# Output-weight remainders on VectorE: one operation of 512 columns or two of 256

## The chip, the cores and the metric

The kernel runs on one core of a Trainium2 chip. The metric is the device time of one execution in microseconds, and the number that counts is the median of the runs. TensorE (PE in the profile) multiplies matrices, VectorE (DVE), ScalarE (ACT) and GpSimd (POOL) do the elementwise work, and SyncE (SP) issues most of the transfers. Every engine works through its own list of instructions in the order in which the program was built, and waits on semaphores for the others.

## The reference

One layer of a model with three parallel mixers. An input of 512 tokens by 1024 channels is normed and projected; the projection feeds a gated linear attention (256 channels), a diagonal state-space mixer (256 channels) and a sparse attention with three branches (512 channels). Their outputs are concatenated and projected back:

```python
h = rmsnorm(x, norm_g[l])
proj = jnp.matmul(h, w_in[l])
...
y_gla = gla_mixer(...)
y_s5 = s5_mixer(...)
y_nsa = nsa_mixer(...)
mix = jnp.concatenate([y_gla, y_s5, y_nsa], axis=-1).astype(x.dtype)
x = x + jnp.matmul(mix, w_out[l])
```

The change lies in the preparation of `w_out`, a 1024 x 1024 float32 matrix, for the last product.

## The kernel before

**Products in three parts.** TensorE takes its operands in a rounded float32 format. To keep accuracy, the kernel splits an operand into a high part (the rounded value) and a low part (the remainder), and sums three products: high times high, high times low, low times high. For the output weights `out_weights` makes the two parts. The matrix lies in eight row blocks k of 128 rows, and each block is handled in two halves of 512 columns (`hf`): SP loads a half into a buffer `wor` (line 1085), ScalarE rounds it into `woh[k]` (line 1086), and the remainder `wor - woh` goes into `wol[k]` (line 1087). The remainder of the first half (`hf` 0) is computed by GpSimd, that of the second half by VectorE; both inputs of the subtraction lie in SBUF. `out_weights(0)` does blocks 0 to 3, `out_weights(1)` blocks 4 to 7, so the line issues eight operations on VectorE and eight on GpSimd. A buffer `wor` comes from a small set of slots that other work uses too; a later load into the slot has to wait until the subtraction has read it.

**Who uses the parts.** `out_first(i)` multiplies the first four row blocks with the mixers' first 512 channels for the 128 tokens of tile i; `out_second(i)` does the last four with the sparse attention's channels and writes the result. Their matmuls stand at line 165, with tiles `pp<-woh,mh`, `pp<-wol,mh`, `pp<-woh,ml` in the first and `moh` in the place of `mh` in the second.

**What runs beside it.** Between 240 and 305 us the kernel works on the attention of the second group of heads. For each unit of it (a tile of 128 queries, a pair of heads, one or two branches): TensorE makes scores `ps`; VectorE takes their maximum `nm` (line 1158); ScalarE takes the exponential into `p` (line 1161); VectorE makes a weighting `dn` from its sum and the branch's gate (lines 1162 and 1163); GpSimd multiplies `p` by `dn` (line 1164; both inputs in SBUF); TensorE transposes `p` into a bank `pt` (line 1182); VectorE or ScalarE, in turn, copies it to `pT` (lines 1186 and 1188); TensorE multiplies `pT` by the values `kvr`. At the end of a pair of tiles VectorE gates the sum into `sng` (line 1213), which frees its bank. In the same stretch a small attention over compressed keys runs, with GpSimd's product at line 1062.

**What sets the order.** Five streams (projection, linear attention, state space, sparse attention, output) are generators, and a string `ORDER` says whose next step is written. The instructions are then placed on the engines' lists by a scheduler that estimates when each would run, so a change of one operation's shape can move others past each other.

Of the kernel before, what the change touches and what calls it, by code (L numbers as in the profile page):

```python
# [8 lines left out]
F32 = mybir.dt.float32  # L9
# [4 lines left out]
OP = mybir.AluOpType  # L14
# [47 lines left out]
def kernel(ctx: ExitStack, tc: tile.TileContext, a: dict, out: bass.AP):  # L62
    nc = tc.nc
    V, S, G, PE = nc.vector, nc.scalar, nc.gpsimd, nc.tensor
# [16 lines left out]
    def al(name, shape, dt=F32, keep=False):  # L81
        size = int(math.prod(shape[1:])) * mybir.dt.size(dt)
        for cls, top, _ in (JOB + CLASSES if any(stack[0] is j for j in job) and not keep and size > 1024 else CLASSES):
            if size <= top and free[cls]:
                slot = free[cls].pop(0)
                t = slots.tile(list(shape), dt, name=name, tag=slot, bufs=1)
                owned[id(t)] = cls, slot, name, t
                if not keep:
                    stack[0][-1].append(t)
                return t  # L90
        raise RuntimeError(f"no slot for {name}: {[(o[0], o[2]) for o in owned.values()]}")
# [23 lines left out]
    @contextmanager  # L115
    def scope():
        st = stack[0]
        st.append([])
        yield
        fr(*[t for t in st.pop() if id(t) in owned])  # L120
# [952 lines left out]
    def out_weights(part):  # L1073
        if part == 0:
            px.close()
            wo = ctx.enter_context(tc.tile_pool(name="wo", bufs=1))
            N["wo"] = [[wo.tile([128, D], F32R, name=f"wo{c}{k}") for k in range(NK)] for c in "hl"]
            N["opart"] = {}
        woh, wol = N["wo"]
        for k in range(4 * part, 4 * part + 4):  # L1080
            for hf in range(2):
                with scope():
                    r = al("wor", (128, 512))
                    c = slice(hf * 512, hf * 512 + 512)
                    nc.sync.dma_start(out=r, in_=a["w_out"][:, k, c])
                    S.activation(woh[k][:, c], r, AF.Copy)
                    (V if hf else G).tensor_tensor(wol[k][:, c], r, woh[k][:, c].bitcast(F32), op=OP.subtract)  # L1087
            yield

    def out_mm(ps, lh, ll, ks, n):  # L1090
# [126 lines left out]
    with scope():  # L1217
# [5 lines left out]
    s5 = Stream(s5_params, s5_in, s5_scan, s5_out_weights, s5_y, s5_glu)  # L1223
    nsa = Stream("cmp_blocks", cmp_mlp, "nsa_q0", "nsa_kv0", (cmp_attn, 0), "nsa_kv1", (attn, 0), "nsa_q1", (cmp_attn, 1), (attn, 1))
    outs = Stream("nsa_gate1", (out_weights, 0), (out_first, 3), (out_first, 2), (out_weights, 1), (out_first, 1), (out_first, 0),
                  "mix11", (out_second, 3), (out_second, 2), "mix10", (out_second, 1), (out_second, 0))
    job.append(outs.stack)
# [108 lines left out]
```

## Time and profile before

| | |
|---|---|
| runs shown | 350.76, 351.85 and 632.46 us, median 351.85 |
| the profiled execution | 348.96 us, of which its span 347.0 us |
| granted TensorE clock | 1.00 over the span |
| busy: PE, VectorE, ScalarE, GpSimd | 333.3, 241.3, 161.9 and 74.7 us |

The profile is one execution, seen by the hardware profiler. Its page names each group of instructions by line, engine, operation, output and inputs. In a timeline a row gives the start, the length, the instruction and, in brackets, how long the engine had been idle before it and whose work ended that. Lengths of one behind another on the same engine overlap a little: the next instruction may start before the record of the one before ends, so what one costs its engine is read from start to start. PE is busy in nearly every slice, but this is a modelled busy time of pipelined matmuls.

### The profile page before, as it was taken

The numbers are of one execution on the slowest core, as the hardware profiler recorded it, in microseconds if no ns is written. First come the engines' busy times: TensorE is split into PE (matmuls) and PEld (weight loads), VectorE is DVE, ScalarE is ACT, GpSimd is POOL, SyncE is SP. The second block draws the span as 40 slices with busy tenths as digits, with TensorE's granted clock in tenths as the row PEclk, the third lists the DMA queues.
The fourth block names the chain that finished last, engine by engine and source line by source line (L and its number), as shares of the span: only waits on it lengthen the run. The fifth ranks groups of instructions, "written<-read, shape, count | busy, mean of one in ns | idle before, by whom it ended". The sixth has DMA issues, their size and how long they took to land.

```text
span 347.0 us, 6782 instructions
## 1 busy us (share of the span) xinstructions
PE 333.3 (96%) x2620; PEld 271.1 (78%) x2620; DVE 241.3 (70%) x502; ACT 161.9 (47%) x355; POOL 74.7 (22%) x74
## 2 busy tenths in 40 slices
PE   8999998999999999999999999999889899899996
PEld 3889987989997767878778877788766687678785
DVE  2839989999995325844759577978998865843422
ACT  3875542358561125622607249634975355732200
POOL 0000232200000000002301041644584335811000
PEclk9999999999999999999999999999999999999999
DMA  6997577133384557621423200121341123500122
GB/s 181 353 358 240 140 233 238 34 117 86 106 258 129 135 161 228 173 56 35 118 72 82 73 0 2 32 53 39 93 124 30 60 63 120 178 7 2 61 91 91
DMA packets 27538, 40.35 MB, mean 116 GB/s; under 512 B 3033, under 2 KB 16738, under 8 KB 27506
## 3 DMA queue, kind: packets, MB, share of 16 engines
q1 hardware_dynamic: 26370, 37.23, 35.7%
q0 software_dynamic: 1136, 2.69, 2.7%
q8 instruction: 20, 0.33, 0.4%
q14 instruction: 12, 0.10, 0.1%
HBM read 33.42 MB, written 3.92 MB: 108 GB/s over the span
## 4 chain that ended last, share of the span: by engine, by line
PE 63%; DVE 18%; DMA 9%; ACT 6%; issue 3%; POOL 1%; SPq 0%; ACTq 0%; DVEq 0%; POOLq 0%
PE pp L165 33%; PE pt L165 14%; PE ps L165 11%; DMA wor<-in_w_out_dram 4%; DVE nm L1158 3%; DVE wol L1087 2%; ACT p L1161 2%; DMA wr<-in_w_kv_dram 2%; PE pt L1182 2%; DMA wr<-in_w_ng_dram 1%; DVE wl L230 1%; DMA xr<-in_xT_dram 1%; DVE pT L1186 1%; DMA wr<-in_w_nq_dram 1%; DVE dn L1163 1%
## 5 line engine op out<-in xcount | busy, mean ns | idle before, releaser
L1164 POOL TENSOR_TENSOR p<-p,dn 128x1024 f32<-128x1024 f32 (+2 forms) x24 | 39.7, 1653 | 48.2 <-DVE dn L1163 42.8
L229 ACT ACTIVATE wh<-wr 128x512 fp32r<-128x512 f32 (+2 forms) x48 | 30.2, 635 | 38.0 <-PE pp L165 13.7
L230 DVE TENSOR_TENSOR wl<-wr,wh 128x512 fp32r<-128x512 f32 (+2 forms) x48 | 34.8, 730 | 18.0 <-ACT wh L229 17.9
L165 PE MATMUL pp<-wh,xh 128*128 128x256 f32 (+2 forms) x160 | 45.6, 288 | 1.5 <-ACT qr L280 1.4
L165 PE MATMUL pp<-wh,xl 128*128 128x256 f32 (+2 forms) x160 | 45.8, 287 | 0.0
L165 PE MATMUL pp<-wl,xh 128*128 128x256 f32 (+2 forms) x160 | 45.7, 286 | 0.0
L1161 ACT ACTIVATE p<-ps,nm 128x512 f32<-128x512 f32 (+3 forms) x64 | 33.2, 532 | 20.1 <-DVE nm L1158 19.1
L165 PE MATMUL pp<-xh,wh 128*128 128x512 f32 x80 | 32.0, 401 | 0.3 <-DVE sgt L285 0.3
L165 PEld LDWEIGHTS pp<-wh,xh 128*128 128x128 f32 x160 | 30.0, 189 | 2.7 <-ACT qr L280 1.6
L165 PE MATMUL pp<-xh,wl 128*128 128x512 f32 x80 | 32.0, 400 | 0.0
L165 PE MATMUL pp<-xl,wh 128*128 128x512 f32 x80 | 32.0, 400 | 0.0
L165 PE MATMUL ps<-kA,qA 128*128 128x512 f32 (+2 forms) x96 | 28.5, 388 | 2.5 <-ACT p L1161 2.5
L165 PEld LDWEIGHTS pp<-wh,xl 128*128 128x128 f32 x160 | 30.1, 188 | 0.7 <-issue 0.6
L165 PEld LDWEIGHTS pp<-wl,xh 128*128 128x128 f32 x160 | 30.2, 189 | 0.4 <-issue 0.2
L1158 DVE TENSOR_REDUCE nm<-ps 128x1 f32<-128x512 f32 (+3 forms) x48 | 27.5, 590 | 3.6 <-PE ps L165 3.5
L165 PE MATMUL pt<-pT,kvr 128*64 128x128 f32 x320 | 22.6, 280 | 2.2 <-DVE pT L1186 2.1
L1182 PE MATMUL pt<-ident,p 128*128 128x128 f32 x160 | 23.4, 278 | 0.5 <-POOL p L1164 0.4
L165 PEld LDWEIGHTS pt<-pT,kvr 128*64 128x64 f32 x320 | 17.0, 136 | 7.4 <-DVE pT L1186 3.4
L1182 PEld LDWEIGHTS pt<-ident,p 128*128 128x128 f32 x160 | 17.5, 141 | 4.5 <-issue 2.4
L165 PEld LDWEIGHTS ps<-kA,qA 128*128 128x128 f32 x96 | 14.8, 190 | 5.6 <-ACT p L1161 4.5
L1020 POOL MEMSET vblk<- 128x512 f32 x1 | 0.5, 524 | 86.0 <-PE pt L165 86.0
L165 PEld LDWEIGHTS pp<-xh,wl 128*128 128x128 f32 x80 | 15.1, 188 | 3.9 <-issue 0.8
(384 smaller groups left out, 758.0 us busy)
## 6 DMA issues: line engine op xcount, KB each, us to landing
w<-in_w_dram SPq DMA_DIRECT2D x16, 256.0 KB, 3.8
wor<-in_w_out_dram SPq DMA_DIRECT2D x16, 256.0 KB, 2.8
xr<-in_xT_dram SPq DMA_DIRECT2D x8, 256.0 KB, 5.9
xn<-in_xn_dram SPq DMA_DIRECT2D x4, 512.0 KB, 7.0
wr<-in_w_kv_dram SPq DMA_DIRECT2D x8, 256.0 KB, 3.8
wr<-in_w_nq_dram SPq DMA_DIRECT2D x8, 256.0 KB, 5.9
wr<-in_w_ng_dram SPq DMA_DIRECT2D x8, 256.0 KB, 3.7
opart<-in_xn_dram SPq DMA_DIRECT2D x4, 512.0 KB, 3.9
```

Source lines behind the costliest of these rows:

```text
L165: PE.matmul(o, lhsT=l, rhs=r, start=start, stop=stop, **kw)
L229: S.activation(hs[qt][:, :, :w], r[:, :, :w], AF.Copy)
L230: V.tensor_tensor(ls[qt][:, :, :w], r[:, :, :w], hs[qt][:, :, :w].bitcast(F32), op=OP.subtract)
L1020: G.memset(vblk, 0.0)
L1087: (V if hf else G).tensor_tensor(wol[k][:, c], r, woh[k][:, c].bitcast(F32), op=OP.subtract)
L1158: V.tensor_reduce(nm[:, e], sv[e], axis=AX.X, op=OP.max, negate=True)
L1161: S.activation(pv[:, e, b], sv[e][:, b], AF.Exp, bias=nm[:, e, b:b + 1], accum_out=dn[:, e, b:b + 1])
L1163: V.tensor_tensor(dn, dn, gates[:, i].rearrange("p (h b) -> p h b", b=3)[:, h:h + 2, 1 + b0:1 + b0 + nb], op=OP.mult)
L1164: G.tensor_tensor(pv, pv, dn[:, :, :, None].to_broadcast([128, 2, nb, n]), op=OP.mult)
L1182: PE.transpose(pb[:, tok(x_)], p[:, e, c:c + 128], ident)
L1186: V.tensor_copy(pt[:, :w], pb[:, :w])
```

## The change

On VectorE the subtraction of a half of 512 columns is written as two operations of 256 columns, the second right behind the first; the values that are computed are the same. GpSimd's eight subtractions stay as they are.

```diff
                     nc.sync.dma_start(out=r, in_=a["w_out"][:, k, c])
                     S.activation(woh[k][:, c], r, AF.Copy)
-                    (V if hf else G).tensor_tensor(wol[k][:, c], r, woh[k][:, c].bitcast(F32), op=OP.subtract)
+                    if hf:
+                        for q in range(2):
+                            c = slice(hf * 512 + q * 256, hf * 512 + q * 256 + 256)
+                            V.tensor_tensor(wol[k][:, c], r[:, q * 256:q * 256 + 256], woh[k][:, c].bitcast(F32),
+                                            op=OP.subtract)
+                    else:
+                        G.tensor_tensor(wol[k][:, c], r, woh[k][:, c].bitcast(F32), op=OP.subtract)
             yield
```

The scheduler places the new operations, and a few others change places. Line numbers from 1087 on rise by six in the changed kernel (1158 becomes 1164), the tile numbers of one and the same step by a few. Three places matter here.

VectorE's list around the third subtraction (row block 2), where `dn` is a weighting and `nm` a maximum; before:

```order
L1163 TENSOR_TENSOR dn_3069<-dn_3069,gates 128x2
L1087 TENSOR_TENSOR wol_3156<-wor,woh_3148 128x512
L1186 COPY pT<-pt_3016 128x512
L1158 TENSOR_REDUCE nm<-ps_3189 128x1
L1162 RECIPROCAL dn_3087<-dn_3087 128x2
L1163 TENSOR_TENSOR dn_3087<-dn_3087,gates 128x2
L1158 TENSOR_REDUCE nm<-ps_3190 128x1
```

and with the change:

```order
L1169 TENSOR_TENSOR dn_3069<-dn_3069,gates 128x2
L1090 TENSOR_TENSOR wol_3156<-wor,woh_3148 128x256 x2
L1192 COPY pT<-pt_3016 128x512
L1164 TENSOR_REDUCE nm<-ps_3192 128x1
L1168 RECIPROCAL dn_3087<-dn_3087 128x2
L1164 TENSOR_REDUCE nm<-ps_3193 128x1
L1169 TENSOR_TENSOR dn_3087<-dn_3087,gates 128x2
```

The two halves stand side by side, and behind them the second maximum has moved ahead of the weighting that GpSimd's product needs.

GpSimd's list around its last subtraction (row block 7), where `p` is the product with the weighting; before:

```order
L1087 TENSOR_TENSOR wol_3160<-wor,woh_3152 128x512
L1164 TENSOR_TENSOR p<-p,dn_3456 128x2x384
L1164 TENSOR_TENSOR p<-p,dn_3493 128x1024
L1087 TENSOR_TENSOR wol_3161<-wor,woh_3153 128x512
L1164 TENSOR_TENSOR p<-p,dn_3631 128x1024
```

and with the change:

```order
L1093 TENSOR_TENSOR wol_3160<-wor,woh_3152 128x512
L1170 TENSOR_TENSOR p<-p,dn_3460 128x2x384
L1093 TENSOR_TENSOR wol_3161<-wor,woh_3153 128x512
L1170 TENSOR_TENSOR p<-p,dn_3497 128x1024
L1170 TENSOR_TENSOR p<-p,dn_3639 128x1024
```

The last subtraction has moved ahead of the first of the two 1024-column products.

TensorE's list at the same time, where `pt<-ident,p` are the transposes of `p`, `pt<-pcT,vb` the first products into a new bank, and `pp` the output products of a tile; before:

```order
L165 MATMUL pt_3129<-pT,kvr_1146 64x128 x6
L1182 MATMUL pt_3652<-ident,p 128x128 x4
L1182 MATMUL pt_3659<-ident,p 128x128 x4
L165 MATMUL pt_3665<-pcT_1894,vb_1811 128x256
L165 MATMUL pt_3665<-pcT_1895,vb_1811 128x256
L165 MATMUL pt_3665<-pcT_1894,vb_1812 128x256
L165 MATMUL pp_3563<-woh_3146,mh 128x512
L165 MATMUL pp_3563<-wol_3154,mh 128x512
```

and with the change:

```order
L165 MATMUL pt_3129<-pT,kvr_1146 64x128 x6
L165 MATMUL pp_3571<-woh_3146,mh 128x512
L165 MATMUL pp_3571<-wol_3154,mh 128x512
L165 MATMUL pp_3585<-woh_3146,mh 128x512
L165 MATMUL pp_3585<-wol_3154,mh 128x512
L1188 MATMUL pt_3660<-ident,p 128x128 x4
L1188 MATMUL pt_3667<-ident,p 128x128 x4
L165 MATMUL pt_3673<-pcT_1894,vb_1811 128x256
```

Four output products have moved ahead of the transposes and of the products into the new bank.

## Rows read from the trace of the kernel before

**Rows 1.** The head of the profile's page: the span, then the busy time of each engine as a share of the span with its number of instructions.

```profile
span 347.0 us, 6782 instructions
...
PE 333.3 (96%) x2620; PEld 271.1 (78%) x2620; DVE 241.3 (70%) x502; ACT 161.9 (47%) x355; POOL 74.7 (22%) x74
```

**Rows 2.** The table by stretches: start and end of the stretch and its length in us, then the busy time (and number of instructions) of PE, the weight loads, DVE, ACT and POOL, the granted TensorE clock as a fraction of full speed, the DMA share and GB/s.

```profile
240.00:305.00 65.00, 59.15 (x473) 47.20 (x473) 53.29 (x102) 39.43 (x122) 36.24 (x24) 1.00 0.31 94
305.00:344.00 39.00, 38.93 (x222) 31.60 (x222) 14.15 (x26) 6.02 (x17) 2.08 (x2) 1.00 0.13 49
```

**Rows 3.** The timeline of PE: start us, length us, engine, line, operation, out<-in, and in brackets the idle time just before with what ended it. The first six rows are waits of PE for VectorE, ScalarE and GpSimd; the last two are the first and the last of four products in a row.

```profile
255.25 0.66 PE L165 MATMUL pt<-pT,kvr 128*64 128x128 f32 x8 [0.49 <-DVE pT L1186]
...
259.79 0.66 PE L165 MATMUL pt<-pT,kvr 128*64 128x128 f32 x8 [1.07 <-DVE pT L1186]
...
266.76 0.63 PE L165 MATMUL ps<-kA,qA 128*128 128x384 f32 x2 [0.54 <-ACT p L1161]
...
291.44 0.88 PE L165 MATMUL pt<-pT,kvr 128*64 128x128 f32 x12 [0.56 <-DVE pT L1186]
...
297.92 0.44 PE L1182 MATMUL pt<-ident,p 128*128 128x128 f32 x2 [0.43 <-POOL p L1164]
...
303.38 0.62 PE L165 MATMUL pt<-pcT,vb 128*128 128x256 f32 x3 [0.37 <-DVE sng L1213]
303.83 0.45 PE L165 MATMUL pp<-woh,mh 128*128 128x512 f32 x1
...
304.58 0.40 PE L165 MATMUL pp<-wol,mh 128*128 128x512 f32 x1
```

**Rows 4.** A piece of the chain of work that ended last: start us, length us, engine, tile, line.

```profile
252.50 1.18 DVE wol L1087
...
253.71 2.81 DMA wor<-in_w_out_dram
...
256.54 0.64 ACT woh L1086
...
257.20 1.93 DVE wol L1087
```

**Rows 5.** The timeline of DVE (columns as in rows 3) at a place where POOL stands still: operations with both inputs in SBUF, one behind the other.

```profile
189.68 0.41 DVE L509 TENSOR_TENSOR ex<-ex,kT 128x256 f32<-128x256 f32 x1
190.02 0.68 DVE L288 SCALAR_TENSOR_TENSOR sgt<-sl_t,sgt 128x512 f32<-128x512 f32 x1
190.62 0.68 DVE L230 TENSOR_TENSOR wl<-wr,wh 128x512 fp32r<-128x512 f32 x1
```

**Rows 6.** The timeline of POOL (columns as in rows 3) where the output weights are split.

```profile
251.84 1.29 POOL L1087 TENSOR_TENSOR wol<-wor,woh 128x512 fp32r<-128x512 f32 x1
253.08 1.49 POOL L1164 TENSOR_TENSOR p<-p,dn 128x512 f32<-128x512 f32 x1
254.77 1.04 POOL L1164 TENSOR_TENSOR p<-p,dn 128x512 f32<-128x512 f32 x1 [0.19 <-DVE dn L1163]
256.69 1.89 POOL L1164 TENSOR_TENSOR p<-p,dn 128x1024 f32<-128x1024 f32 x1 [0.89 <-DVE dn L1163]
258.54 1.72 POOL L1087 TENSOR_TENSOR wol<-wor,woh 128x512 fp32r<-128x512 f32 x1
...
262.85 1.90 POOL L1164 TENSOR_TENSOR p<-p,dn 128x1024 f32<-128x1024 f32 x1 [0.19 <-DVE dn L1163]
...
286.28 1.47 POOL L1164 TENSOR_TENSOR p<-p,dn 128x768 f32<-128x768 f32 x1 [0.99 <-ACT p L1161]
...
296.11 1.76 POOL L1164 TENSOR_TENSOR p<-p,dn 128x768 f32<-128x768 f32 x1 [0.18 <-DVE dn L1163]
298.64 1.89 POOL L1164 TENSOR_TENSOR p<-p,dn 128x1024 f32<-128x1024 f32 x1 [0.78 <-DVE dn L1163]
300.49 1.28 POOL L1087 TENSOR_TENSOR wol<-wor,woh 128x512 fp32r<-128x512 f32 x1
301.93 2.21 POOL L1164 TENSOR_TENSOR p<-p,dn 128x1024 f32<-128x1024 f32 x1 [0.17 <-DVE dn L1163]
```

**Rows 7.** The timeline of DVE (columns as in rows 3) in the same stretch.

```profile
252.42 1.25 DVE L1087 TENSOR_TENSOR wol<-wor,woh 128x512 fp32r<-128x512 f32 x1
...
259.06 0.68 DVE L1186 COPY pT<-pt 128x512 f32<-128x512 f32 x1
...
260.44 0.16 DVE L1163 TENSOR_TENSOR dn<-dn,gates 128x2 f32<-128x2 f32 x1
...
262.25 0.43 DVE L1163 TENSOR_TENSOR dn<-dn,gates 128x2 f32<-128x2 f32 x1
...
263.80 1.49 DVE L1087 TENSOR_TENSOR wol<-wor,woh 128x512 fp32r<-128x512 f32 x1
...
284.66 1.19 DVE L1087 TENSOR_TENSOR wol<-wor,woh 128x512 fp32r<-128x512 f32 x1
...
295.86 0.68 DVE L1087 TENSOR_TENSOR wol<-wor,woh 128x512 fp32r<-128x512 f32 x1
...
300.93 0.85 DVE L1163 TENSOR_TENSOR dn<-dn,gates 128x4 f32<-128x4 f32 x1
301.71 0.68 DVE L1087 TENSOR_TENSOR wol<-wor,woh 128x512 fp32r<-128x512 f32 x1
```

**Rows 8.** The timeline of ScalarE (columns as in rows 3): the last load of output weights for POOL as it is rounded.

```profile
298.69 0.63 ACT L1086 ACTIVATE woh<-wor 128x512 fp32r<-128x512 f32 x1 [0.50 <-DMA wor<-in_w_out_dram]
```

## The prediction, made before the changed kernel was run

> **What bounds the kernel.** The page's head comes first: PE is busy for 333.3 of 347.0 us, VectorE for 241.3, POOL for 74.7 [rows 1]. That says TensorE, but the matter is decided by stretches, so the second view is the table by stretches, cut where the edit lies. From 240 to 305 us, where the output weights are split, PE is busy for 59.15 of 65 us and VectorE for 53.29; from 305 to 344 PE is idle for 0.07 of 39 us, at a granted clock of 1.00 in both [rows 2], the upper of its two levels. So the end is PE work alone, and an edit of VectorE can shift the end only through the 5.85 us of PE idle before 305. The third view, PE's timeline, names who ends that idle time: pT copies of VectorE, exponentials that wait for VectorE's maxima, a product of POOL, a gating of VectorE [rows 3]. What stands on VectorE ahead of those is what counts, and the edited line is among it: the chain of waits runs through it twice within 5 us, by way of the load that its end sets free [rows 4].
>
> The fourth view lays VectorE and POOL side by side. An operation of 512 columns with both inputs in SBUF is 0.68 us long and the next starts 0.60 us behind it [rows 5]. The edited line takes 1.25, 1.93 and 1.49 us at 252, 257 and 263 us [rows 7]. Each time POOL is in the middle of an operation, and VectorE ends about 0.55 us after POOL's end: 256.69 + 1.89 = 258.58, VectorE's end 257.20 + 1.93 = 259.13; 262.85 + 1.90 = 264.75, VectorE's end 265.29 [rows 6, 7]. The two exclude each other. It holds the other way too: POOL's operations right behind, at 253.08, 258.54 and 301.93, take 1.49, 1.72 and 2.21 us where their forms take 1.04, 1.28 and 1.89 [rows 6].
>
> **The change, term by term.** Eight subtractions of 512 columns become sixteen of 256. No byte, PE matmul or transfer is added; SP's list has the same transfers in the same order. I call the eight places pair 1 to pair 8; they start near 247, 252, 257, 264, 285, 290, 296 and 302 us.
>
> *Without POOL.* A 256-column operation is 0.41 us long, and the next starts 0.34 us after it; a 512-column one costs 0.60 [rows 5]. Two halves cost 0.68, which is 0.08 more for a pair. The Trainium skill (VectorE: DVE Perf Modes, "The DRAIN you can't avoid") has the next operation wait until the pipe is empty, which speaks against the change: an estimate by that page is two full lengths of 0.41 against one of 0.68, so 0.14 for a pair and 0.5 us more over the eight. The trace contradicts it: the 0.41 us operation at 189.68 is followed at 190.02 [rows 5].
>
> *With POOL waiting.* This is the term with two far ends. If an operation of POOL already waits when the first half ends, either VectorE keeps its turn for the second half (price 0.08), or POOL goes in between and the second half waits for a whole POOL operation. This trace shows no pair of VectorE operations with a POOL operation waiting at their seam. The nearest rows are the mirror image. POOL's 256.69 operation ends at 258.58 and its next one, at 258.54, is already there; VectorE, waiting since 257.20, went in between, and POOL's second lost 0.44 us. The same happened at 253.08, for 0.45 us [rows 6, 7]. So a turn is given up between two operations of one engine and the waiting one gets it. I take that value for the other direction, and keep 0.08 as the lower end. The Trainium skill (SBUF — State Buffer, "Who interferes with whom") says that such a pair of instructions holds the shared access for one whole instruction and that issue order decides; by it the seam is a place where it can change hands. That VectorE waits for whole POOL operations agrees with the 1.93 us row; what happens at a seam of VectorE's, no run here shows yet.
>
> Pair by pair, then:
> - Pair 2. POOL's 253.08 operation waits from the start; the seam is near 253.4. The second half waits for its 1.04 us. Behind it on VectorE stands the pT copy for which PE waits at 255.25 with 0.49 idle [rows 3], and the next load of weights starts at the pair's end [rows 4]. All of it is on the path: **+1.04**.
> - Pair 3. POOL's 258.54 subtraction waits; 1.28 by the form at 300.49 [rows 6]. Behind the pair stands the copy at 259.06 [rows 7], for which PE idles 1.07 at 259.79 [rows 3]: **+1.28**.
> - Behind pair 3 the scheduler puts a maximum ahead of a weighting dn (260.44), which then comes about 0.5 late (0.60 for an operation of 512 columns [rows 5]). POOL's next product starts that much later, holds the next dn (262.25) longer, so POOL's 262.85 operation and pair 4 behind it (263.80) are late too [rows 6, 7], and so is the exponential that PE waits for at 266.76 [rows 3]: **+0.5**.
> - Pairs 1, 4, 5, 6 have no POOL operation waiting at the seam. Pair 5 is nearest: over at 285.85 [rows 7], while POOL's next starts at 286.28 after 0.99 idle [rows 6]. Pair 6 is ahead of the copy of the 291.44 wait [rows 3]. 4 × 0.08 = **+0.3**.
> - Pair 7 runs from 295.86; its seam is at 296.20, and POOL's product starts at 296.11 and asks a little later: a tie. I take **+0.1**, through POOL's product, for which PE waits at 297.92. If POOL wins the tie, VectorE loses 1.47, of which PE sees about 0.95.
> - The stretch of pair 8. POOL's last subtraction now goes ahead of a 1024-column product. It can start when its weights are rounded, 298.69 + 0.63 = 299.3 [rows 8], and ends at 300.6; the product (1.89) then lasts to 302.5 instead of 300.53. The weighting dn at 300.93 ended at 301.78 and is now held to 302.5; pair 8 starts there, not at 301.71. Its seam is at 302.8, POOL's next product (dn's) waits by then, takes 1.89, and the second half ends at 305.0 where pair 8 ended at 302.39: 2.6 late. PE's wait at 303.38 is for the gating behind pair 8 [rows 3]. Against this PE now has four products of output weights ahead of that wait, (304.58 − 303.83) / 3 = 0.25 each, 1.0 in all [rows 3]. **+1.6**.
>
> Sum: 1.04 + 1.28 + 0.5 + 0.3 + 0.1 + 1.6 = **4.8 us**. The profiled execution took 348.96 us, so 353.8. The undisturbed runs shown stand 1.8 and 2.9 us above it (350.76 and 351.85, the latter the median); with the lower of these, 353.8 + 1.8 = **355.6 us**.
>
> **The rivals.**
> - *VectorE keeps its turn* over both halves. For it: nothing but that the second half has no wait of its own and follows within 0.34 us. Against: the mirror rows. Then 8 × 0.08 = 0.6, plus 0.5 behind pair 3, and in the last stretch pair 8 ends at 303.2, 0.8 late, against 1.0 of PE work brought forward: −0.2. Sum +0.9: 349.9, in runs 351.7.
> - *Slower by over 2%.* Place: pairs 5 and 7. If the pairs before make VectorE so late that POOL's product is already waiting at these two seams, pair 7 gives 0.95 more and pair 5 one more 768-column product, 1.47. The point from which it decides: pair 5 at least 0.4 us later against POOL than now, pair 7 by any amount. 4.8 + 0.95 + 1.47 = 7.2: 356.2, in runs 358.0. Against it: POOL's products hang on VectorE's dn and shift along.
> - *Slightly faster: only the order counts.* PE's four products fill its idle time in full (−1.0), the swap behind pair 3 is absorbed by the wait for the loads, and the halves cost 0.6: 348.6, in runs 350.4. Against it: VectorE is busy for 53 of those 65 us [rows 2], so little is absorbed.
> - That the halves are not issued is excluded: the order of instructions has them side by side.
>
> **The numbers.** POOL goes between: 0.55. VectorE keeps its turn: 0.33. More seams caught: 0.07. Faster by order: 0.05. The range takes in the second and most of the third and fourth, with the 1 us by which the runs shown differ: 350.2 to 358.8; the likeliest case alone has 353.5 to 357.5 (pair 2 and 3 alone, up to pair 7 lost). About 2%, 7.0 us, is what a measurement of this kernel can tell from no change. PE's idle of 5.85 us is less than that, so faster by over 2% is nearly excluded (0.02). Slower: most of the third case and a little of the first (0.08). Within 2%: 0.90.
>
> **What would show it.** In the new trace, pairs 2, 3 and 8 have a second half of 1.3 to 2.2 us and no stretched POOL operation beside them; PE's wait for the pT copy grows to about 1.5 after pair 2 and 2.3 after pair 3. If VectorE keeps its turn, all second halves are 0.41 us long and POOL's 1.49 and 1.72 stay. If POOL's product runs past 302 us and PE's four products come at about 302, the step on the last stretch is right. I am wrong if PE's idle time before 305 us stays near 5.9, or if it grows at places that no half touches.

## The result, and the profile after

The changed kernel took 356.19 us (median of 4 runs, 353.52 to 358.08) against 352.15 us for the kernel before: a ratio of 1.0133, 95% interval 1.0093 to 1.0172, or 4.7 us (3.3 to 6.1). That is slower, but by less than 2%. The forecast was 355.6 us, within 2%. The 352.15 us is the median of four runs, one of which took 632.46 us; the ratio leaves that one out. In the further comparison described below the ratio was 1.0147 (1.0115 to 1.0178).

The page of the changed kernel, its head:

```profile
span 356.3 us, 6793 instructions
...
PE 337.2 (95%) x2620; PEld 273.3 (77%) x2620; DVE 246.7 (69%) x510; ACT 161.9 (45%) x355; POOL 73.8 (21%) x74
```

It has 11 instructions more, eight of them on VectorE, and a span 9.3 us longer than that of [rows 1]. This execution lies 1.9 us above the median of its kernel, so its parts are read apart below. The waits of PE, as totals (engine, line, whom it waited for: us in total, times, longest), show where the change acts:

```profile
PE pt L165 <- DVE pT L1192: 5.0, 4, 2.1
...
PE pt L165 <- DVE sng L1219: 1.9, 1, 1.9
```

Before, the waits for the copies pT were 0.49, 1.07 and 0.56 us, and the one for the gating sng 0.37 [rows 3]. PE's timeline (columns as in rows 3) has the places; its first row stands ahead of them all:

```profile
241.09 0.88 PE L165 MATMUL pt<-pT,kvr 128*64 128x128 f32 x12
...
258.90 0.66 PE L165 MATMUL pt<-pT,kvr 128*64 128x128 f32 x8 [1.30 <-DVE pT L1192]
...
264.57 0.66 PE L165 MATMUL pt<-pT,kvr 128*64 128x128 f32 x8 [2.07 <-DVE pT L1192]
...
304.69 0.88 PE L165 MATMUL pt<-pT,kvr 128*64 128x128 f32 x12 [1.04 <-DVE pT L1192]
...
312.20 0.62 PE L165 MATMUL pt<-pcT,vb 128*128 128x256 f32 x3 [1.92 <-DVE sng L1219]
```

The four waits lie behind pairs 2, 3, 7 and 8. These are the pairs on VectorE's timeline; the length is that of both halves, from the start of the first to the end of the second:

```profile
255.34 2.17 DVE L1090 TENSOR_TENSOR wol<-wor,woh 128x256 fp32r<-128x256 f32 x2
...
261.02 2.90 DVE L1090 TENSOR_TENSOR wol<-wor,woh 128x256 fp32r<-128x256 f32 x2 [0.85 <-ACT woh L1086]
...
301.42 2.02 DVE L1090 TENSOR_TENSOR wol<-wor,woh 128x256 fp32r<-128x256 f32 x2
...
308.76 2.45 DVE L1090 TENSOR_TENSOR wol<-wor,woh 128x256 fp32r<-128x256 f32 x2
```

and GpSimd's timeline has the operations beside them:

```profile
256.00 1.22 POOL L1170 TENSOR_TENSOR p<-p,dn 128x512 f32<-128x512 f32 x1
...
262.25 1.38 POOL L1093 TENSOR_TENSOR wol<-wor,woh 128x512 fp32r<-128x512 f32 x1
...
301.67 1.49 POOL L1170 TENSOR_TENSOR p<-p,dn 128x768 f32<-128x768 f32 x1 [0.19 <-DVE dn L1169]
...
308.99 1.94 POOL L1170 TENSOR_TENSOR p<-p,dn 128x1024 f32<-128x1024 f32 x1 [0.17 <-DVE dn L1169]
```

In [rows 6] the same four took 1.49, 1.72, 1.76 and 2.21 us; in [rows 7] and [rows 4] the whole subtractions took 1.25, 1.93, 0.68 and 0.68. So at four of the eight seams the delay has changed sides: GpSimd's operation is shorter by 0.27 to 0.34 us, which fits that it waits for half of VectorE's work only, and VectorE's pair is longer by 0.9 to 1.8 us, which fits that its second half waits for all of GpSimd's. The experiments test this reading.

### The profile page after: what moved, and what is told of

It reads as the page before. It is cut to its first block, busy times and chain, and to the rows that moved or that the text cites. A ratio compares the mean times of both kernels' runs of the same rounds, so it can differ in the third digit from the quotient of the medians.

```text
span 356.3 us, 6793 instructions
## 1 busy us (share of the span) xinstructions
PE 337.2 (95%) x2620; PEld 273.3 (77%) x2620; DVE 246.7 (69%) x510; ACT 161.9 (45%) x355; POOL 73.8 (21%) x74
## 4 chain that ended last, share of the span: by engine, by line
PE 51%; DVE 21%; DMA 15%; ACT 7%; issue 4%; SPq 1%; ACTq 0%; DVEq 0%
PE pp L165 29%; PE pt L165 12%; PE ps L165 8%; ACT p L1167 3%; DVE wol L1090 3%; DMA wor<-in_w_out_dram 3%; DMA wr<-in_w_nq_dram 2%; DMA small<-in_small_dram 2%; DVE wl L230 2%; DMA xn<-in_xn_dram 2%; DVE nm L1164 2%; DMA xr<-in_xT_dram 2%; PE pt L1188 2%; DMA dmr<-in_dm_dram 1%; DMA wr<-in_w_ng_dram 1%
## 5 line engine op out<-in xcount | busy, mean ns | idle before, releaser
L1170 POOL TENSOR_TENSOR p<-p,dn 128x1024 f32<-128x1024 f32 (+2 forms) x24 | 38.9, 1620 | 53.5 <-DVE dn L1169 46.7
L165 PEld LDWEIGHTS pt<-pT,kvr 128*64 128x64 f32 x320 | 17.3, 138 | 10.2 <-DVE pT L1192 6.6
L165 PEld LDWEIGHTS ps<-kA,qA 128*128 128x128 f32 x96 | 15.1, 194 | 5.4 <-ACT p L1167 4.0
```

What stands on the lines that cost most here:

```text
L165: PE.matmul(o, lhsT=l, rhs=r, start=start, stop=stop, **kw)
L1170: G.tensor_tensor(pv, pv, dn[:, :, :, None].to_broadcast([128, 2, nb, n]), op=OP.mult)
```

## The experiments

The theory ("turns"): where a GpSimd operation is waiting at the seam, it goes in between the halves, and the second half waits for the whole of it. The rivals: the new order of the instructions does the harm, or the mere number of operations does. The first four runs cut some pairs alone; `k` is the number of the pair less one. Their edit, with the condition of the first of them:

```diff
-                    (V if hf else G).tensor_tensor(wol[k][:, c], r, woh[k][:, c].bitcast(F32), op=OP.subtract)
+                    if hf and k in (0, 3, 4, 5):
+                        for q in range(2):
+                            c = slice(hf * 512 + q * 256, hf * 512 + q * 256 + 256)
+                            V.tensor_tensor(wol[k][:, c], r[:, q * 256:q * 256 + 256], woh[k][:, c].bitcast(F32),
+                                            op=OP.subtract)
+                    else:
+                        (V if hf else G).tensor_tensor(wol[k][:, c], r, woh[k][:, c].bitcast(F32), op=OP.subtract)
```

**Pairs 1, 4, 5 and 6 alone.** Expected:

> Only pairs 1, 4, 5 and 6 are split, those behind which no POOL operation waited at the seam; the other four stay whole. TensorE's list differs from before by one swap of transposes, the other lists by nothing but the halves and one swap of a copy and a reciprocal. Turn theory (POOL takes the turn at a seam where it already waits): no second half waits, a pair costs 0.08 us more, 0.3 us in all, ratio 1.000 to 1.002. Overhead theory (an operation more costs what it costs wherever it stands): half of the change's loss of about 4 us, ratio 1.005 or more. Order theory (the loss comes from the operations that the scheduler moved): 1.000.

Measured: ratio 1.0018 (0.9988 to 1.0048), so +0.6 us (−0.4 to 1.7), not to be told from none. No second half waited: the four lasted 0.41 or 0.42 us, and the longest of all eight, 1.23, was a first half. Eight of the sixteen halves are in this kernel, so their mere number does not make the 4.7 us.

**Pair 2 alone.** Condition `hf and k == 1`. Expected:

> Only pair 2 is split; every list is in the order of before. Turn theory: between the halves POOL's 512-column product runs, VectorE is 1.0 us later behind the pair, PE's wait for the pT copy grows from 0.49 to about 1.5 us, and the time rises by 1.0 us (ratio 1.003). Keep theory (VectorE keeps its turn) and order theory: 0.1 us, POOL's stretched 1.49 us product stays.

Measured: ratio 1.0031 (1.0001 to 1.0062), +1.1 us (0.0 to 2.2). The second half lasted 1.26 us, GpSimd's product between the halves 1.22 instead of 1.49, and PE waited 1.20 us for the copy behind it instead of 0.49 [rows 3]. The order of the instructions is that of the kernel before, so the delay is none of the order's. Behind the pair the wait at pair 3 shrank from 1.07 to 0.62 us: VectorE's subtraction there, now later, lasted 1.44 us instead of 1.93.

**Pair 3 alone.** Condition `hf and k == 2`. Expected:

> Only pair 3 is split; every list is in the order of before. Turn theory: POOL's subtraction of 1.28 us runs between the halves, PE's wait for the pT copy grows from 1.07 to about 2.3 us, and the time rises by 1.3 us (ratio 1.004). Keep theory and order theory: 0.1 us, and POOL's subtraction beside it stays at 1.7 us.

Measured: ratio 1.0042 (1.0016 to 1.0068), +1.5 us (0.6 to 2.4). Here too the order is unchanged. The halves lasted 1.70 and 1.48 us: the first waited for the end of one GpSimd operation, the second for the whole of the next. PE's wait for the copy was 2.20 us instead of 1.07.

**Pair 8 alone.** Condition `hf and k == 7`. Expected:

> Only pair 8 is split; POOL's, TensorE's and VectorE's lists are in the order of before (ScalarE does one rounding ahead of a small exponential). Turn theory: POOL's 1024-column product, 1.89 us, runs between the halves, the gating behind the pair and PE's wait for it come up to 1.9 us later (wait 0.37 to about 2.2), ratio 1.003 to 1.006. Keep theory and order theory: 0.1 us.

Measured: ratio 1.0099 (1.0068 to 1.0131), +3.5 us (2.4 to 4.6). The halves lasted 0.41 and 2.11 us; PE waited 2.16 us for the gating instead of 0.37. This run does not have the four output products ahead of that wait. The wait accounts for 1.8 us. The rest came behind it in this execution, with a lower clock: PE is 308.03 − 303.38 = 4.65 us behind the kernel before when the wait ends, and the span is 353.1 − 347.0 = 6.1 us longer. PE's timeline behind the wait:

```profile
308.03 1.01 PE L165 MATMUL pt<-pcT,vb 128*128 128x256 f32 x3 [2.16 <-DVE sng L1219]
308.84 0.63 PE L165 MATMUL pp<-woh,mh 128*128 128x512 f32 x1
...
310.12 0.63 PE L165 MATMUL pp<-wol,mh 128*128 128x512 f32 x1
```

The same products took 0.40 us, 0.25 from start to start, in [rows 3]; here it is 0.63 and 0.43. The granted clock of the stretch from 308 to 310 us was 0.50, and 1.00 again from 312. How much of the other runs' time is the clock's isn't known, since only this execution has a trace.

**The turn by itself.** A kernel of its own, told in the expectation, of which there is one execution:

> This kernel computes none of the reference: it copies two tiles of the input and runs six phases, one after the other, each of eight subtractions of 512 columns on VectorE: (a) whole, alone; (b) as two halves, alone; (c) whole, while GpSimd runs eight subtractions of 512 columns of its own, all in SBUF; (d) as halves beside the same; (e) as four quarters of 128 columns beside the same; (f) as halves with one input in PSUM beside the same. Both theories: (a) 0.60 us per start, (b) 0.34 per half, (f) halves of 0.4 us as if alone, GpSimd at about 1.04 to 1.28. Turn theory (a waiting GpSimd operation goes in at each seam between two VectorE operations): in (c) every operation of VectorE and GpSimd takes its turn, VectorE one start per 1.9 us; in (d) one HALF per GpSimd operation, so the first eight halves are 1.6 us apart and GpSimd is finished after about four pairs; in (e) one QUARTER per GpSimd operation, GpSimd finished after two subtractions. Rival (the pair keeps the turn because its second half follows without a wait of its own): in (d) a pair per GpSimd operation, halves by turns 1.6 and 0.4 us, GpSimd finished only after the eighth pair. Rival (a share of the port's time, not turns): all phases with GpSimd stretched by one factor and no operation whole.

The groups of its instructions by shape, costliest first: the names in the rows are v for VectorE's results and g for GpSimd's, then wa, ha, wp, hp, qp and cp for the phases (a) to (f). Behind the bar stand the busy time and the mean ns of one:

```profile
L39 DVE TENSOR_TENSOR vqp<-iaqp,b 128x128 f32<-128x128 f32 x32 | 15.1, 545 | 0.0
L39 DVE TENSOR_TENSOR vhp<-iahp,b 128x256 f32<-128x256 f32 x16 | 14.0, 945 | 0.0
L33 POOL TENSOR_TENSOR gwp<-iawp,b 128x512 f32<-128x512 f32 x8 | 13.4, 1713 | 19.9 <-DVE iawp L27 19.9
...
L33 POOL TENSOR_TENSOR ghp<-iahp,b 128x512 f32<-128x512 f32 x8 | 11.3, 1445 | 1.5 <-DVE iahp L27 1.5
L33 POOL TENSOR_TENSOR gqp<-iaqp,b 128x512 f32<-128x512 f32 x8 | 10.2, 1312 | 4.2 <-DVE iaqp L27 4.2
L33 POOL TENSOR_TENSOR gcp<-iacp,b 128x512 f32<-128x512 f32 x8 | 9.8, 1260 | 6.4 <-DVE iacp L27 6.4
L39 DVE TENSOR_TENSOR vha<-iaha,b 128x256 f32<-128x256 f32 x16 | 5.5, 416 | 0.0
L39 DVE TENSOR_TENSOR vcp<-iacp,ps 128x256 f32<-128x256 f32 x16 | 5.4, 413 | 0.0
L39 DVE TENSOR_TENSOR vwa<-iawa,b 128x512 f32<-128x512 f32 x8 | 4.9, 684 | 0.0
```

GpSimd's eight operations took 13.4 us beside whole ones (wp), 11.3 beside halves (hp) and 10.2 beside quarters (qp): 1.68, 1.41 and 1.28 us for one. VectorE's cost alone is 4.9 / 8 = 0.61 a whole one, 5.5 / 16 = 0.34 a half, and (15.1 − 10.2) / 24 = 0.20 a quarter, by the 24 quarters that are left when GpSimd has finished. Take that away, and about 1.07 us is left each time. So there is one operation of VectorE, whatever its width, to each of GpSimd's. That is the order that the turn theory expected; the times are shorter than its 1.9 and 1.6 us. The halves' own row agrees: eight at 1.41 and eight at 0.34 make 14.0 us. A pair that kept its turn would have held GpSimd until the eighth pair; it was finished after eight halves. Sharing by time falls as well: GpSimd gives up one operation's length each time, not a factor.

With one input in PSUM (cp) neither engine notices the other: 0.41 us a half as alone, and 1.26 for one of GpSimd's. The Trainium skill (SBUF — State Buffer, "Who interferes with whom") has it that a VectorE instruction with at most one input in SBUF does not contend with GpSimd, and (same page, "SBUF: two separate sides") that with two inputs there, against a GpSimd operation that reads SBUF, whichever starts first holds the shared ports for its whole instruction; the phases agree with both. The Trainium skill's rule on draining (VectorE: DVE Perf Modes, "The DRAIN you can't avoid"), taken by itself as in the prediction, would give a half alone its full length, 0.41 us; the section makes an exception for a next operation that is not held, which starts earlier. The 0.34 of phase (b), like [rows 5], agrees with the exception and not with the bare rule.

**Pair 3 cut unevenly.** The edit of pair 3, with `for lo, up in ((0, 448), (448, 512)):` in the place of the two halves. Expected:

> Only pair 3 is cut, unevenly, into 448 and 64 columns; the order on every engine is that of the kernel before. Turn theory: the price is GpSimd's whole operation (about 1.3 us, its wol of 512 columns), whatever is behind the seam: the 64-column rest takes about 1.4 us instead of 0.2, PE's wait for the copy behind it is 2.1 to 2.3 us instead of 1.07, and the time is that of the even cut, 1.2 to 1.6 us over the kernel before. Rival (the price is the time VectorE needs for the second half, or is shared out by width): below 0.5 us, not to be told from none.

Measured: ratio 1.0031 (1.0006 to 1.0055), +1.1 us, with PE's wait for the copy at 2.21 us. The interval does not tell this from the even cut, and takes in 0.5. The row of the tile decides:

```profile
L1090 DVE TENSOR_TENSOR wol<-wor,woh x2: 1280/1568/1857, 259.8 to 261.6; 128x448 fp32r<-128x448 f32 x1, 128x64 fp32r<-128x64 f32 x1
```

The operation of 64 columns lasted 1.28 us. What the second part costs goes by GpSimd's operation, not by its own width.

**Pairs 2 and 3 together.** Condition `hf and k in (1, 2)`; a maximum and a weighting dn behind pair 3 change places as in the changed kernel. Expected:

> Pairs 2 and 3 together, which brings with it the exchange of a maximum and a weighting dn behind pair 3 that the changed kernel has too. By the prediction's terms +1.04, +1.28 and +0.5: 2.8 us over the kernel before. If the two pairs alone count, as measured singly, +1.3 and +1.5: about 2.8 without anything for the exchange; but pair 2 alone left pair 3 less held up, so if that gain stays, 2.0 to 2.4. PE's waits for the copies: about 1.2 behind pair 2 and 2.1 behind pair 3, the next wait for an exponential 0.3 to 0.6.

Measured: ratio 1.0049 (1.0020 to 1.0077), +1.7 us, below all three of the expected figures, though the interval reaches to 2.7. In this execution pair 3 lost nothing at its seam: it lasted 1.44 us, with PE's wait for the copy at 0.62, because GpSimd, 0.41 us idle for its rounded weights, began its subtraction only at 262.48, when VectorE's second half, begun at 262.27, already ran. The price of pair 3 thus hangs on who is ready first. The exchange behind it did show:

```profile
270.77 0.62 PE L165 MATMUL ps<-kA,qA 128*128 128x384 f32 x2 [1.01 <-ACT p L1167]
```

PE's wait for that exponential was 0.54 before [rows 3], and 0.54 with pair 2 alone and 0.55 with pair 3 alone, where the order is the old one.

**Pair 7 alone.** Condition `hf and k == 6`; the scheduler then moves the four output products as in the changed kernel. Expected:

> Only pair 7 is cut; that brings the scheduler's move of four products of output weights on PE ahead of its wait for the gating, as in the changed kernel, without pair 8. Tie theory (GpSimd asks late, as predicted): both halves 0.41 us, and PE saves up to 1.0 us of products but only as far as it waited (0.37 at that gating): -0.3 to +0.2 us. Lost-tie theory (as in the trace of the changed kernel): the second half waits for the product of GpSimd, 1.5 us, GpSimd's product takes 1.49 instead of 1.76, PE's wait for the copy behind it grows by 0.9 to 1.0: +0.6 to +1.1 us.

Measured: ratio 1.0028 (0.9999 to 1.0057), +1.0 us (0.0 to 2.0), which the runs alone hardly tell from none. The trace does: the tie was lost, with halves of 0.41 and 1.68 us, GpSimd's product 1.49 instead of 1.76, PE's wait for the copy behind it 1.04. The products brought forward did not pay here: the wait for the gating fell from 0.37 to 0.15 us, but a new one of 0.75 for `ml` came behind it. No run has the new order of this stretch without a cut, so its own share was not measured.

**The changed kernel again.** No edit. Expected:

> The changed kernel itself once more, beside the others. What the parts gave singly (0.6 for the quiet pairs, 1.1 pair 2, 1.5 pair 3, 1.0 pair 7, 3.5 pair 8) adds up to 7.7 us, but pairs 2 and 3 together gave 1.7 instead of 2.6, and the products brought forward are in both of the last two. If the prices only overlap in this way: 4 to 5.5 us over the kernel before. Two points differ from execution to execution by the turn theory: whether GpSimd's subtraction already waits at the seam of pair 3 (PE then idles 2.1 us for the copy, otherwise about 0.6), and whether TensorE's clock falls to 0.50 behind its longest waits; the runs should therefore lie up to 3 us apart.

Measured: 357.21 against 351.84 us, ratio 1.0147 (1.0115 to 1.0178), +5.2 us (4.0 to 6.3). Its profiled execution had a granted clock of 1.00 throughout. Both open points went otherwise than in pieces: pair 3 lost its turn (it lasted 2.97 us), unlike in the run of pairs 2 and 3, and the clock stayed up, unlike in the run of pair 8. This is the execution in which the terms can be read without the clock; rows of its PE timeline:

```profile
240.06 0.88 PE L165 MATMUL pt<-pT,kvr 128*64 128x128 f32 x12
...
257.86 0.66 PE L165 MATMUL pt<-pT,kvr 128*64 128x128 f32 x8 [1.27 <-DVE pT L1192]
...
263.54 0.66 PE L165 MATMUL pt<-pT,kvr 128*64 128x128 f32 x8 [2.15 <-DVE pT L1192]
...
271.04 0.61 PE L165 MATMUL ps<-kA,qA 128*128 128x384 f32 x2 [1.08 <-ACT p L1167]
...
295.97 0.88 PE L165 MATMUL pt<-pT,kvr 128*64 128x128 f32 x12 [0.76 <-DVE pT L1192]
...
302.19 0.44 PE L1188 MATMUL pt<-ident,p 128*128 128x128 f32 x2 [0.17 <-POOL p L1170]
303.67 0.88 PE L165 MATMUL pt<-pT,kvr 128*64 128x128 f32 x12 [1.04 <-DVE pT L1192]
...
306.38 0.88 PE L165 MATMUL pt<-pT,kvr 128*64 128x128 f32 x12
307.19 0.50 PE L165 MATMUL pp<-woh,mh 128*128 128x512 f32 x1
...
308.22 1.03 PE L1188 MATMUL pt<-ident,p 128*128 128x128 f32 x8
311.17 0.63 PE L165 MATMUL pt<-pcT,vb 128*128 128x256 f32 x3 [1.92 <-DVE sng L1219]
...
318.53 0.60 PE L165 MATMUL pt<-pcT,vb 128*128 128x256 f32 x3
```

and, of the kernel before, the rows that answer to the first and to two of the last:

```profile
238.24 0.88 PE L165 MATMUL pt<-pT,kvr 128*64 128x128 f32 x12
...
301.11 0.88 PE L165 MATMUL pt<-pT,kvr 128*64 128x128 f32 x12
...
311.80 0.59 PE L165 MATMUL pt<-pcT,vb 128*128 128x256 f32 x3
```

They are used in the next section.

**All low halves on VectorE.** `V` in the place of `(V if hf else G)`. Expected:

> All low halves on VectorE, whole operations of 512 columns, none on GpSimd; the scheduler reorders the stretch. By the exclusion theory VectorE takes eight more starts of 0.60 (4.8 us) and is freed of the waits for GpSimd's subtractions (1.25, 1.93 and 1.49 us fall towards 0.68 where the partner was a subtraction), GpSimd is freed of ten us. If VectorE's queue ahead of TensorE's waits decides: +1 to +3 us over the kernel before. If GpSimd's turns decide: -2 to 0.

Measured: ratio 0.9953 (0.9928 to 0.9979), −1.7 us (−2.5 to −0.7). VectorE has eight operations more, and the kernel is faster, which is what was expected if GpSimd's turns decide. The order changed too, so the gain can't be put down to the turns.

**All low halves on GpSimd.** `G` in the same place. Expected:

> All low halves on GpSimd, whole, none on VectorE; the scheduler reorders the stretch. VectorE is freed of eight operations that cost it 0.60 to 1.93 us each (7.4 us beyond what stands in no one's way), GpSimd takes eight more of 1.28 us, so its products of probabilities can come up to 1.3 us later. If VectorE's queue decides: -1 to -2 us. If GpSimd's products decide: +1 to +3 us, with TensorE's waits for GpSimd's product above 1 us.

Measured: ratio 1.0288 (1.0247 to 1.0328), +10.1 us: the sign of the second case, and more than three times its size. The longest wait of PE is not for a product of probabilities:

```profile
320.36 0.79 PE L165 MATMUL pp<-woh,mh 128*128 128x512 f32 x1 [4.57 <-ACT mh L1104]
```

GpSimd's last two subtractions start at 318.31 and 319.61 us. The rounding of `mh`, for which PE waits, begins at 319.68, as the first of them ends. Five of the loads of output weights are issued only from 305.04 us on, where the last one before went out by 296.9. Why they are so late was not taken apart, and the run says little about turns.

**GpSimd's subtractions in halves, VectorE's whole.** The edit above with `if not hf:` and `G` in the place of `V`. Expected:

> The mirror image: VectorE's subtractions stay whole and GpSimd's eight are cut into two of 256 columns each; the scheduler reorders some operations on both engines. Turn theory: a waiting VectorE operation goes in at GpSimd's seam, so it waits for half a subtraction (about 0.6 us) instead of a whole one (1.28), and GpSimd's second half loses the 0.4 to 0.6 us of VectorE's operation. Pair 3's row of 1.88 to 1.93 us falls to about 1.3: -0.3 to -1 us over the kernel before, unless the new order of VectorE eats it. Rival (seams only cost): 0 to +1 us.

Measured: 348.72 against 351.84 us, ratio 0.9918 (0.9887 to 0.9949), −2.9 us (−4.0 to −1.8). Of the kernels tried it is the fastest, ahead of both that were compared. VectorE's timeline at pairs 2 and 3, whole here, and GpSimd's beside it:

```profile
253.01 0.70 DVE L1093 TENSOR_TENSOR wol<-wor,woh 128x512 fp32r<-128x512 f32 x1
...
257.17 0.68 DVE L1093 TENSOR_TENSOR wol<-wor,woh 128x512 fp32r<-128x512 f32 x1
```

```profile
252.43 1.88 POOL L1090 TENSOR_TENSOR wol<-wor,woh 128x256 fp32r<-128x256 f32 x2
...
257.42 2.19 POOL L1170 TENSOR_TENSOR p<-p,dn 128x1024 f32<-128x1024 f32 x1 [0.88 <-DMA wor<-in_w_out_dram]
```

At pair 2 the mirror image holds: VectorE's operation went in at GpSimd's seam and took 0.70 us where it had taken 1.25 [rows 7], and GpSimd's two halves took 1.88 us where an undisturbed two take 1.42 (start 239.38 in the same trace). Pair 5 shows the same: 0.69 us on VectorE instead of 1.19. At pair 3 no seam was needed: VectorE's subtraction starts ahead of GpSimd's product here, and the product waits for it (2.19 instead of 1.89). The gain is larger than expected, and how much of it is the seams and how much the order was not taken apart.

## Why the prediction was right, point by point

The rows of the changed kernel's second execution, set against those of the kernel before ([rows 3] and the three above), give each term as the growth of the lag between two points on PE. The last column has the growth between the same two points in the traces of the kernels in which only some pairs are cut (pairs 1, 4, 5 and 6; pair 2; pair 3; pairs 2 and 3; pair 7):

| point on PE | before | changed | lag | growth | term of the sum | cut alone |
|---|---|---|---|---|---|---|
| ahead of all eight | 238.24 | 240.06 | 1.82 | | | |
| behind pairs 1 and 2 | 255.25 | 257.86 | 2.61 | +0.79 | 1.04 (pair 2) | +0.06 (pair 1), +0.71 (pair 2) |
| behind pair 3 | 259.79 | 263.54 | 3.75 | +1.14 | 1.28 | +1.14, cut unevenly +1.14 |
| behind pair 4 and the exchange | 266.76 | 271.04 | 4.28 | +0.53 | 0.5 (exchange) | +0.08 (pair 4), +0.46 (exchange, with pairs 2 and 3) |
| behind pairs 5 and 6 | 291.44 | 295.97 | 4.53 | +0.25 | 0.3 (with pairs 1 and 4) | +0.22 |
| at GpSimd's product beside pair 7 | 297.92 | 302.19 | 4.27 | −0.26 | | −0.26 |
| behind pair 7 | 301.11 | 306.38 | 5.27 | +1.00 | 0.1 | +1.00 |
| behind the last stretch | 311.80 | 318.53 | 6.73 | +1.46 | 1.6 | none |

The growth adds up to 4.91 us where the sum had 4.8, and down to pair 7 the pieces measured singly make up the whole, to within 0.03 us a row. The first 1.82 us lie ahead of the change and belong to the execution, not to the kernel: at that point pair 2 alone is 4.05 us late and pair 3 alone 1.60, with the order of before.

- *GpSimd goes between* was right, and the mirror rows on which it rested were the right ones to look at. The rival that VectorE keeps its turn falls with the isolated phases, the one that only the order counts with pairs 2 and 3, each cut alone.
- *The price of a turn* was a little too high: whole forms of 1.04, 1.28 and 1.89 us were taken. The isolated run gives 1.07 for the form of 1.28. In the second execution pair 8 lasted 2.44 us where [rows 7] has 0.68; less the 0.08 of a second operation that is 1.68 for the form of 1.89. A turn costs some 0.2 us less than the record of the operation is long. So PE's waits behind pairs 2 and 3 came to 1.27 and 2.15 us where the text had 1.5 and 2.3. And GpSimd's operations beside pairs 2, 3 and 8, said to come unstretched, stayed 0.05 to 0.18 us above their forms.
- *Pairs 1, 4, 5 and 6*: the price of 0.08 a pair is what PE shows, 0.06 at pair 1 and 0.08 at pair 4. At pairs 5 and 6 it can't be told: PE's lag grew by 0.22 with them cut, and by 0 to 0.30 in kernels in which they are whole.
- *Pair 7* is the step that failed: "a tie. I take **+0.1**". GpSimd won in all three profiles in which the pair is cut, and VectorE's row was 2.02 us instead of 0.68. PE saw 1.00 at the copy behind it, close to the 0.95 that the text kept for a lost tie, but had gained 0.26 just before, since GpSimd's product came sooner: 0.74 in all. GpSimd's row began at 296.11 [rows 6] and the seam was put at 296.20; the text let the product ask later than its row begins, and it was there already.
- *The last stretch* came as told: four products ahead at 307.19 us (301.9 without the lag of 5.27), worth 308.22 − 307.19 = 1.03, and the gating's wait ends 311.17 − 303.38 − 5.27 = 2.52 late, where the text had 2.6.
- *The size in the runs* was right by help of errors that cancel, which is luck: 0.64 too little at pair 7, 0.55 too much elsewhere. In the first execution the lag is 241.09 − 238.24 = 2.85 ahead of the pairs and 9.3 at the end: it grew by 6.4 us and not 4.9. The clock adds the 1.5 between them, as the last section shows, and no term of the sum had it. How much of the 4.7 us in the runs is the clock's was not measured.

## What to carry to other kernels

Before an operation of VectorE with both inputs in SBUF is cut, look for a GpSimd operation that waits at the seam: each such seam costs VectorE nearly that whole operation (here 1.07 us for a record of 1.28), however narrow the rest. On the engine whose turns are waited for (here GpSimd, with operations of 1.3 to 1.9 us) the same cut let VectorE in earlier; whether that alone gained time was not separated from the new order. And to price a change in a trace, match rows of the engine that sets the end and read how the lag grows from one to the next: the first execution's 9.3 us of longer span held 2.9 that came before the change and 1.5 of clock.

## What was not expected

TensorE's clock. Before, it was granted at 1.00 over the span; in the first execution of the changed kernel it fell to 0.50, the lower of its levels (1.2 GHz), for two short stretches behind PE's waits of 2.07 and 1.92 us. The table by stretches (columns as in rows 2):

```profile
266.00:268.00 2.00, 2.00 (x9) 1.06 (x7) 1.28 (x3) 2.00 (x5) 1.89 (x1) 0.50 0.04 14
...
310.00:312.00 2.00, 0.28 (x3) 0.04 (x1) 2.00 (x3) 0.42 (x3) 0.93 (x1) 1.00 0.03 10
312.00:314.00 2.00, 1.80 (x7) 1.42 (x8) 1.34 (x3) 2.00 (x11) 0.00 (x0) 0.88 0.00 0
314.00:316.00 2.00, 2.00 (x6) 1.53 (x5) 0.34 (x2) 0.27 (x2) 1.04 (x1) 0.50 0.00 0
```

At the second of them the output products take 0.43 us from start to start (six intervals from 313.65 to 316.21) instead of 0.23 (in the second execution, eighteen from 312.11 to 316.32). What that cost is read from the lag between PE's gating wait and the end: in the second execution it shrank by 7.79 − 6.73 = 1.06, the four products brought forward; in the first it grew from 312.20 − 303.38 = 8.82 to 9.3. The gain of the products is gone, and the difference between the two executions is 1.5 us in all. The first stretch at 0.50 cost nothing at the end: PE had been going to wait 1.08 us for the exponential there, as in the second execution, and in the first has no such wait.

In that second execution the same idle time of 1.92 us is followed by the full clock:

```profile
310.00:312.00 2.00, 0.83 (x4) 0.65 (x5) 2.00 (x5) 1.45 (x7) 0.00 (x0) 1.00 0.00 0
...
314.00:316.00 2.00, 2.00 (x10) 1.63 (x9) 0.69 (x1) 0.00 (x0) 0.87 (x1) 1.00 0.00 0
```

Pair 3 alone had a wait of 2.20 us, and its granted clock stayed at 1.00 from 262 to 268 us; behind the 2.16 us of pair 8 alone it was 0.50.

So a wait on the path can cost more than its length, from execution to execution. Of the changed kernel's four runs the fastest, 353.52 us, had a mean granted clock of 1.00, the others 0.986 to 0.99; of the six runs of the second comparison the fastest, 355.52, had 1.00, the others 0.986 to 0.995. Where the clock fell in the runs without a trace isn't known, and it need not be at these waits: with pair 7 alone it was 0.50 from 60 to 62 us, far ahead of all pairs. Why the clock falls behind one such wait and not behind the other stayed open; no run here was made to settle it.
